# Gate, up and conv projections of a split-float32 decoder kernel: two activation parts in one 512-column matmul

## The chip, the cores and the metric

One core of a Trainium2 chip. The metric is device microseconds of one execution. The kernel is compared with itself after one change.

## The reference, cut to what matters

The model is two layers of [half SwiGLU FFN, parallel token mixing, half SwiGLU FFN] over 256 tokens of width 1024, all in float32, with one RMSNorm at the end.

```
def swiglu(h, wg, wu, wd):
    return (jax.nn.silu(h @ wg) * (h @ wu)) @ wd
...
for l in range(2):
    x = x + 0.5 * swiglu(rms_norm(x, ffn1_norm[l]), ffn1_wg[l], ffn1_wu[l], ffn1_wd[l])
    z = rms_norm(x, mix_norm[l]) @ w_in[l]     # retention, block attention, conv: a, gate
    ...                                        # u = a * sigmoid(gate), then the depthwise conv
    x = x + mix @ w_out[l]
    x = x + 0.5 * swiglu(rms_norm(x, ffn2_norm[l]), ffn2_wg[l], ffn2_wu[l], ffn2_wd[l])
return rms_norm(x, final_norm)
```

The FFN is 2816 wide, that is 22 tiles of 128; the conv branch has 256 channels and a gate of 256.

## The kernel before, in words

**Products.** Each float32 operand is split into a float32r high part and a float32r remainder ("hi" and "lo"), and a product is the sum of three passes: hi times hi, hi times lo, lo times hi. All three accumulate in PSUM.

**Weights.** They arrive as one stream of units of up to 1 MB, in the order of use, through three "raw" buffers filled from SyncE's queue (L125). `pump` splits the next half unit: ScalarE copies it to a "whi" piece (L145) and VectorE subtracts to get "wlo" (L146). Ten pieces of each exist (`WBUFS`). `take` hands pieces to the products and `free` returns them.

**Order.** TensorE runs in the order in which the code emits its work. `tick` follows each group of products; it pumps one half unit and advances side chains, which are generators that wait for some number of ticks before their next TensorE work. In the stretches where the order is not written out by hand (`ordered(False)`: most of an FFN, and the mixing from the conv projections on) a planner places the work of ScalarE and VectorE; in the others they too run as emitted.

**An FFN** (`ffn`, four times). `first_pair` (L407) makes the first two tiles with the activations as the stationary operand and 512 columns of weights streaming (L201 to L203). Its result is transposed (L401) into a bank of the tag "tr" called `pt` and split from there (L404). Then ten pairs of `single` (L416): 20 tiles, each with a gate half and an up half of 8 steps over the inner dimension. A step is `mm3w` (L205 to L209): three matmuls of 256 columns, with the weights (whi, whi, wlo) as the stationary operand and the activations (hThi, hTlo, hThi) streaming. Gate and up are written to the two column halves of one bank of the tag "mm", which has two banks, as has "tr"; "acc" has four. Behind the up half ScalarE takes the Silu of the gate from PSUM (L428), VectorE multiplies by the up half from PSUM (L429), and the product is split (L430, in L196 and L197). From the third tile pair on, each pair of `single` is followed by two `down` blocks for tiles of the pair before the last (L433 to L445): 512 columns of weights streaming past the split product. The last four tiles go through `down` in a tail (L469 to L473), and the residual is added (L475).

**The mixing** (`mix`, twice). It starts with two attention projections (`chunk`, L488, 384 columns each), then `glu` (L658) makes the conv branch's gate and value with `mm3w`, into "acc" banks: two rounds of 8 steps for each of two channel tiles. Gate: Sigmoid on ScalarE (L674); value: a product on VectorE into `u` (L676). Then 31 taps of depthwise convolution run on VectorE (L686, L688) under the other projections, and TensorE transposes the result (L694). The output projection is `outp` (L768 to L781), 512 columns of weights streaming.

**Activations.** `new_hT` (L361) makes two tiles, "hThi" and "hTlo", each 128 x 8 x 256; `norm_T` (L345) fills them from transposes. The last norm (`Final`, L899) uses one buffer of each tag for its two row tiles (L905, L906).

Of the kernel before, what the change touches and what calls it, by code (L numbers as in the profile page):

```python
# [11 lines left out]
F32 = mybir.dt.float32  # L12
F32R = mybir.dt.float32r
BF16 = mybir.dt.bfloat16
I32 = mybir.dt.int32
AF = mybir.ActivationFunctionType
OP = mybir.AluOpType
AX = mybir.AxisListType
PSUM = bass.MemoryType.PSUM

D = 1024
S = 256
P = 128
L = 2
KT = D // P
NT = S // P
# [4 lines left out]
HW = H * HD  # L31
# [12 lines left out]
NVEC = OFF_BT + 2 * L  # L44


# Float32 products run as three float32r passes: every operand is split exactly into a
# float32r high part and a float32r remainder, and hi*hi + hi*lo + lo*hi accumulate in PSUM.
#
# Weights arrive as one stream of units in the order of use. `pump` splits the next half unit  # L50
# into a rotating set of hi/lo pieces, `take` hands pieces to the products, `free` gives them
# back. TensorE runs in emission order; `tick` follows every group of products and advances
# the side chains (generators that yield the number of ticks, or the condition, to wait for
# before their next TensorE work), so that their latency hides behind the products.
class Kernel:
    def __init__(self, ctx, tc, a, out):
        self.tc, self.nc, self.a, self.out = tc, tc.nc, a, out
# [24 lines left out]
    def bank(self, tag, bufs):  # L82
        return self.ps.tile([P, 512], F32, tag=tag, bufs=bufs, name=self.name(tag))
# [118 lines left out]
        mm(out, ah, wl, start=False, stop=False)  # L202
        mm(out, al, wh, start=False, stop=stop)  # L203

    def mm3w(self, out, wh, wl, xh, xl, start, stop):  # L205
        mm = self.nc.tensor.matmul
        mm(out, wh, xh, start=start, stop=False)  # L207
        mm(out, wh, xl, start=False, stop=False)  # L208
        mm(out, wl, xh, start=False, stop=stop)  # L209

    def load(self, name, shape, dt=F32, eng=None):
        t = self.const.tile(list(shape), dt, tag=name, name=name)
# [146 lines left out]
        return g  # L359

    def new_hT(self):  # L361
        hi = self.act.tile([P, KT, S], F32R, tag="hThi", bufs=2, name=self.name("hThi"))
        lo = self.act.tile([P, KT, S], F32R, tag="hTlo", bufs=2, name=self.name("hTlo"))
        return hi, lo

    def projA(self, ps, t, hT, pieces, n, free):
        kk = KT // len(pieces)
# [11 lines left out]
    def ffn(self, f, cur, nxt):  # L379
        nc = self.nc  # L380
        hT = cur.hT
        ys = [[self.acc() for _ in range(2)] for _ in range(NT)]
        with self.tc.tile_pool(name=f"ffn{f}", bufs=1) as fp:
            hf = {}

            def new_hf(j):
                hi = fp.tile([P, S], F32R, tag="hfh", bufs=TAIL + 4, name=self.name("hfh"))
                lo = fp.tile([P, S], F32R, tag="hfl", bufs=TAIL + 4, name=self.name("hfl"))
                hf[j] = (hi, lo)
                return hf[j]  # L390

            def new_sh():
                return [fp.tile([P, 256], F32, tag=x, bufs=2, name=self.name(x)) for x in "sh"]
# [20 lines left out]
                    self.spawn(gated(t, ps, pt))  # L414

            def single(j):  # L416
                ps = self.mmb()
                s, h = new_sh()
                for gu in range(2):
                    (w,) = self.take(1)  # L420
                    wh, wl = [x.rearrange("p (k n) -> p k n", k=KT) for x in w]
                    for k in range(KT):
                        self.mm3w(ps[:, gu * S:(gu + 1) * S], wh[:, k], wl[:, k], hT[0][:, k], hT[1][:, k], k == 0, k == KT - 1)
                        if k == 3:
                            self.tick()
                    self.free()
                    if gu == 1:
                        nc.scalar.activation(s, ps[:, 0:S], AF.Silu)  # L428
                        nc.vector.tensor_tensor(h, s, ps[:, S:2 * S], op=OP.mult)  # L429
                        self.split(*new_hf(j), h)  # L430
                    self.tick()

# [17 lines left out]
            for p in range(1, FT // 2):  # L450
                single(2 * p)
                single(2 * p + 1)
                if p == 1:
                    self.need(f"pair{f}")
                if p > 1:
                    for j in (2 * p - 4, 2 * p - 3):
                        (w,) = self.take(1)
                        for t in range(NT):
                            down(j, t, w)
                            if t == 1:  # L460
                                self.free()
                            self.tick()
                if f == 0 and p == 2:
                    self.setup_late()
                if f == 0 and p == 4:
                    self.spawn(self.tables())
# [12 lines left out]
    def mix(self, l, cur, nxt):  # L479
        nc, a = self.nc, self.a  # L480
        hT = cur.hT
        mT = self.new_hT()
        with self.tc.tile_pool(name=f"mix{l}", bufs=1) as mp:

            def tl(tag, shape, bufs=1):
                return mp.tile(shape, F32, tag=tag, bufs=bufs, name=self.name(tag))

            def chunk(w, t, free):  # L488
                ps = self.mmb()
                self.projA(ps, t, hT, w, HW, free)  # L490
                return ps[:, :HW]
# [166 lines left out]
            def glu():  # L658
                for i in range(2):
                    w = [[x.rearrange("p (k n) -> p k n", k=4) for x in hl] for hl in self.take(2)]  # L660
                    ps = [self.acc()[:, :S] for _ in range(2)]
                    for k in range(KT):
                        wh, wl = w[k // 4]
                        for ct in range(2):
                            cs = slice(ct * P, (ct + 1) * P)
                            self.mm3w(ps[ct], wh[:, k % 4, cs], wl[:, k % 4, cs], hT[0][:, k], hT[1][:, k], k == 0, k == KT - 1)
                        if k % 4 == 3:
                            self.free()
                        if k % 2:
                            self.tick()  # L670
                    for ct in range(2):
                        g = sg[:, ct * S:(ct + 1) * S]
                        if i == 0:
                            nc.scalar.activation(g, ps[ct], AF.Sigmoid)  # L674
                        else:
                            nc.vector.tensor_tensor(u[:, ct, pad:], g, ps[ct], op=OP.mult)  # L676

            def conv():
                for j in range(TAPS):
# [43 lines left out]
            pad = TAPS - 1  # L723
            sg = tl("sg", [P, 512])
            u = tl("u", [P, 2, pad + S])
# [15 lines left out]
            w = self.take(4)  # L741
# [4 lines left out]
            w = self.take(4)  # L746
            for t in range(NT):
                self.spawn(rot(chunk(w, t, t == 1), t, rqT, "rq"))
            w = self.take(4)
            for t in range(NT):  # L750
                self.spawn(rot(chunk(w, t, t == 1), t, rkT, "rk"))
            w = self.take(4)
            rv = [values("rv", chunk(w, t, t == 1)) for t in range(NT)]
            w = self.take(4)
# [3 lines left out]
            for t in range(NT):  # L758
                ps = chunk(w, t, t == 1)
                v = tl("rg", [P, HW], 2)  # L760
# [4 lines left out]
            mm = nc.tensor.matmul  # L765
# [88 lines left out]
class Into:  # L854
# [9 lines left out]
    def state(self, t):  # L864
        k = self.k
        if t == 0:
            self.hT = k.new_hT()
        return {"tile": lambda: k.act.tile([P, D], F32, tag="xr", bufs=1, name=k.name("xr"))}
# [30 lines left out]
class Final(Into):  # L899
# [2 lines left out]

    def state(self, t):
        k = self.k
        tag = "hThi" if t == 0 else "hTlo"  # L905
        return {"tile": lambda: k.act.tile([P, KT * S], F32, tag=tag, bufs=2, name=k.name("y"))[:, :D]}  # L906

    def finish(self, t, n):
        k = self.k
# [67 lines left out]
```

## Time and profile before

| | |
|---|---|
| median of 3 runs | 1013.67 us (1013.66 to 1014.0) |
| span of the profiled execution | 1013.2 us |
| its own time | not recorded beside the span; the median lies 0.5 us above the span |
| matmuls, and weight loads | 6656 each |
| read from memory | 178.74 MB, 177 GB/s over the span |

The profile is one execution. PE is TensorE's matmuls, PEld its weight loads, DVE VectorE, ACT ScalarE, POOL GpSimd, SP SyncE. A row "L207 PE MATMUL mm<-hThi,whi" is an instruction of line 207 that writes a tile of tag mm from hThi and whi. Matmuls are pipelined, so the duration of one row is longer than the distance to the next one's start; the distance between starts is what a matmul costs in a stream. Times on the timeline are microseconds from the span's start.

### The profile page before, as it was taken

How to read it: one execution, taken by the hardware profiler on the slowest of the kernel's cores; microseconds unless marked ns; L12 is line 12 of the kernel's file. 1: busy time of each engine (PE TensorE's matmuls, PEld its weight loads, DVE VectorE, ACT ScalarE, POOL GpSimd, SP SyncE). 2: the span in 40 equal slices, each digit the busy share in tenths (PEclk: the TensorE clock that was granted, in tenths of full speed). 3: DMA queues.
4: the chain of work that ended last, by engine and by line, in shares of the span. 5: the costliest groups of instructions: out<-in, count | busy, mean ns of one | idle time of the engine just before them, and what ended most of it. 6: DMA issues, size and time to landing. Idle time of an engine off the chain costs nothing.

```text
span 1013.2 us, 16088 instructions
## 1 busy us (share of the span) xinstructions
PE 993.9 (98%) x6656; PEld 920.0 (91%) x6656; DVE 625.2 (62%) x864; ACT 483.2 (48%) x736; POOL 66.0 (7%) x109
## 2 busy tenths in 40 slices
PE   5999999999999999999999999999999999999997
PEld 4999999898998999999889999998989889999995
DVE  6875555469976755555575555546699676555542
ACT  5644444356554644444364444444565455444432
POOL 1010000021140000000000000002101400000000
PEclk9999999999999999999999999999999999999999
DMA  9955554436541755545446455543535346555511
GB/s 304 340 191 202 169 202 150 146 118 201 180 167 66 299 196 173 202 169 197 175 172 219 171 194 181 185 148 136 186 136 195 139 155 240 187 188 177 199 42 42
DMA packets 28729, 180.83 MB, mean 178 GB/s; under 512 B 3440, under 2 KB 3824, under 8 KB 10480
## 3 DMA queue, kind: packets, MB, share of 16 engines
q1 hardware_dynamic: 27360, 176.07, 48.9%
q10 hardware_dynamic: 1296, 3.74, 1.0%
q8 instruction: 52, 0.85, 0.3%
q14 instruction: 21, 0.17, 0.0%
HBM read 178.74 MB, written 1.05 MB: 177 GB/s over the span
## 4 chain that ended last, share of the span: by engine, by line
PE 94%; DMA 2%; DVE 2%; ACT 1%; issue 1%; POOL 0%; SPq 0%; POOLq 0%; ACTq 0%; DVEq 0%
PE mm L207 15%; PE mm L209 15%; PE mm L208 15%; PE acc L445 8%; PE acc L441 8%; PE acc L442 8%; PE mm L201 5%; PE mm L203 4%; PE mm L202 4%; PE tr L349 1%; DMA raw<-in_win 1%; PE acc L582 1%; PE acc L632 1%; PE acc L209 1%; PE acc L207 1%; PE acc L208 1%
## 5 line engine op out<-in xcount | busy, mean ns | idle before, releaser
L146 DVE TENSOR_TENSOR wlo<-raw,whi 128x1024 fp32r<-128x1024 f32 (+2 forms) x348 | 403.7, 1172 | 271.6 <-ACT whi L145 271.3
L145 ACT ACTIVATE whi<-raw 128x1024 fp32r<-128x1024 f32 (+2 forms) x348 | 347.7, 1011 | 294.9 <-PE mm L208 179.8
L207 PE MATMUL mm<-hThi,whi 128*128 128x256 f32 x1280 | 362.5, 283 | 0.0
L209 PE MATMUL mm<-hThi,wlo 128*128 128x256 f32 x1280 | 362.0, 283 | 0.0
L208 PE MATMUL mm<-hTlo,whi 128*128 128x256 f32 x1280 | 362.0, 283 | 0.0
L208 PEld LDWEIGHTS mm<-hTlo,whi 128*128 128x128 f32 x1280 | 245.3, 192 | 1.7
L207 PEld LDWEIGHTS mm<-hThi,whi 128*128 128x128 f32 x1280 | 245.2, 192 | 1.6
L209 PEld LDWEIGHTS mm<-hThi,wlo 128*128 128x128 f32 x1280 | 245.3, 192 | 0.0
L441 PE MATMUL acc<-whi,hfh 128*128 128x512 f32 x352 | 139.4, 396 | 0.0
L442 PE MATMUL acc<-wlo,hfh 128*128 128x512 f32 x352 | 138.6, 394 | 0.0
L445 PE MATMUL acc<-whi,hfl 128*128 128x512 f32 x352 | 115.7, 395 | 0.0
L201 PE MATMUL mm<-whi,hThi 128*128 128x384 f32 (+1 forms) x288 | 106.1, 368 | 0.5 <-ACT whi L145 0.5
L202 PE MATMUL mm<-wlo,hThi 128*128 128x384 f32 (+1 forms) x288 | 100.5, 349 | 0.5 <-DVE wlo L146 0.5
L203 PE MATMUL mm<-whi,hTlo 128*128 128x384 f32 (+1 forms) x288 | 100.6, 349 | 0.0
L196 ACT ACTIVATE hfh<-h 128x256 fp32r<-128x256 f32 x80 | 33.4, 418 | 100.1 <-DVE h L429 100.0
L445 PEld LDWEIGHTS acc<-whi,hfl 128*128 128x128 f32 x352 | 66.1, 188 | 15.1
L442 PEld LDWEIGHTS acc<-wlo,hfh 128*128 128x128 f32 x352 | 66.3, 188 | 14.0
L441 PEld LDWEIGHTS acc<-whi,hfh 128*128 128x128 f32 x352 | 66.6, 189 | 13.6
L201 PEld LDWEIGHTS mm<-whi,hThi 128*128 128x128 f32 x288 | 54.4, 189 | 5.3 <-issue 1.3
L202 PEld LDWEIGHTS mm<-wlo,hThi 128*128 128x128 f32 x288 | 54.4, 189 | 3.5 <-DVE wlo L146 1.3
L688 DVE SCALAR_TENSOR_TENSOR ac<-u,vec,ac 128x256 f32<-128x256 f32 x120 | 57.1, 529 | 0.0
L203 PEld LDWEIGHTS mm<-whi,hTlo 128*128 128x128 f32 x288 | 54.1, 188 | 2.7 <-DVE hTlo L197 0.2
(145 smaller groups left out, 712.8 us busy)
## 6 DMA issues: line engine op xcount, KB each, us to landing
raw<-in_wgb SPq DMA_DIRECT2D x80, 1024.0 KB, 4.8
raw<-in_wd SPq DMA_DIRECT2D x44, 1024.0 KB, 4.8
raw<-in_win SPq DMA_DIRECT2D x28, 768.0 KB, 4.4
raw<-in_wout SPq DMA_DIRECT2D x8, 1024.0 KB, 4.7
raw<-in_wga SPq DMA_DIRECT2D x6, 1024.0 KB, 4.8
raw<-in_wcv SPq DMA_DIRECT2D x4, 1024.0 KB, 4.7
raw<-in_wga SPq DMA_DIRECT2D x8, 256.0 KB, 7.1
g<-in_fgain ACTq DMA_DIRECT2D x3, 512.0 KB, 3.4
```

The lines of the kernel that those rows point to most:

```text
L145: nc.scalar.activation(hi[:, c], src, AF.Copy)
L146: nc.vector.tensor_tensor(lo[:, c], src, hi[:, c].bitcast(F32), op=OP.subtract)
L201: mm(out, ah, wh, start=start, stop=False)
L202: mm(out, ah, wl, start=False, stop=False)
L203: mm(out, al, wh, start=False, stop=stop)
L207: mm(out, wh, xh, start=start, stop=False)
L208: mm(out, wh, xl, start=False, stop=False)
L209: mm(out, wl, xh, start=False, stop=stop)
L441: mm(ys[t][h], hi[:, ts], wh[:, n], start=first, stop=False)
L442: mm(ys[t][h], hi[:, ts], wl[:, n], start=False, stop=False)
L445: mm(ys[t][h], lo[:, ts], wh[:, n], start=False, stop=last)
L688: nc.vector.scalar_tensor_tensor(ac[ct], us, wj, ac[ct], op0=OP.mult, op1=OP.add)
```

## The change

A step over the inner dimension is now `mm2w`: one matmul of 512 columns that streams both activation parts past whi, into both column halves of a bank, and one of 256 columns that streams the high part past wlo, into the first half. The low half of the bank is added to the first half outside TensorE: `joined` copies it to SBUF on ScalarE and adds on VectorE. Gate and up take a bank each, gate of tag "mm" and up of tag "tr"; `glu` uses whole "acc" banks. High and low parts of the activations become one tile, and the last norm's two row tiles one tile of the same tag.

```diff
-    def mm3w(self, out, wh, wl, xh, xl, start, stop):
+    def mm2w(self, out, wh, wl, x, start, stop):
         mm = self.nc.tensor.matmul
-        mm(out, wh, xh, start=start, stop=False)
-        mm(out, wh, xl, start=False, stop=False)
-        mm(out, wl, xh, start=False, stop=stop)
+        mm(out, wh, x, start=start, stop=False)
+        mm(out[:, :S], wl, x[:, 0], start=False, stop=stop)
+
+    def joined(self, new, ps):
+        lo, v = new(), new()
+        self.nc.scalar.activation(lo, ps[:, S:], AF.Copy)
+        self.nc.vector.tensor_tensor(v, lo, ps[:, :S], op=OP.add)
+        return v
...
     def new_hT(self):
-        hi = self.act.tile([P, KT, S], F32R, tag="hThi", bufs=2, name=self.name("hThi"))
-        lo = self.act.tile([P, KT, S], F32R, tag="hTlo", bufs=2, name=self.name("hTlo"))
-        return hi, lo
+        both = self.act.tile([P, KT, 2, S], F32R, tag="hT", bufs=2, name=self.name("hT"))
+        return both[:, :, 0], both[:, :, 1], both
...
             def single(j):
-                ps = self.mmb()
                 s, h = new_sh()
-                for gu in range(2):
+                for gu, bank in enumerate((self.mmb, self.trb)):
+                    ps = bank()
                     (w,) = self.take(1)
                     wh, wl = [x.rearrange("p (k n) -> p k n", k=KT) for x in w]
                     for k in range(KT):
-                        self.mm3w(ps[:, gu * S:(gu + 1) * S], wh[:, k], wl[:, k], hT[0][:, k], hT[1][:, k], k == 0, k == KT - 1)
+                        self.mm2w(ps, wh[:, k], wl[:, k], hT[2][:, k], k == 0, k == KT - 1)
                         if k == 3:
                             self.tick()
                     self.free()
-                    if gu == 1:
-                        nc.scalar.activation(s, ps[:, 0:S], AF.Silu)
-                        nc.vector.tensor_tensor(h, s, ps[:, S:2 * S], op=OP.mult)
+                    v = self.joined(lambda: fp.tile([P, S], F32, tag="part", bufs=4, name=self.name("part")), ps)
+                    if gu == 0:
+                        nc.scalar.activation(s, v, AF.Silu)
+                    else:
+                        nc.vector.tensor_tensor(h, s, v, op=OP.mult)
                         self.split(*new_hf(j), h)
                     self.tick()
...
             def glu():
...
-                    ps = [self.acc()[:, :S] for _ in range(2)]
+                    ps = [self.acc() for _ in range(2)]
...
-                            self.mm3w(ps[ct], wh[:, k % 4, cs], wl[:, k % 4, cs], hT[0][:, k], hT[1][:, k], k == 0, k == KT - 1)
+                            self.mm2w(ps[ct], wh[:, k % 4, cs], wl[:, k % 4, cs], hT[2][:, k], k == 0, k == KT - 1)
...
                         g = sg[:, ct * S:(ct + 1) * S]
+                        v = self.joined(lambda: tl("w", [P, HW], 5)[:, :S], ps[ct])
                         if i == 0:
-                            nc.scalar.activation(g, ps[ct], AF.Sigmoid)
+                            nc.scalar.activation(g, v, AF.Sigmoid)
                         else:
-                            nc.vector.tensor_tensor(u[:, ct, pad:], g, ps[ct], op=OP.mult)
+                            nc.vector.tensor_tensor(u[:, ct, pad:], g, v, op=OP.mult)
...
     def state(self, t):
         k = self.k
-        tag = "hThi" if t == 0 else "hTlo"
-        return {"tile": lambda: k.act.tile([P, KT * S], F32, tag=tag, bufs=2, name=k.name("y"))[:, :D]}
+        if t == 0:
+            self.y = k.act.tile([P, NT, D], F32, tag="hT", bufs=2, name=k.name("y"))
+        return {"tile": lambda: self.y[:, t]}
```

## Rows read from the trace of the kernel before

**Rows 1.** The page's head: span, then busy us, share and instructions.

```profile
span 1013.2 us, 16088 instructions
...
PE 993.9 (98%) x6656; PEld 920.0 (91%) x6656; DVE 625.2 (62%) x864; ACT 483.2 (48%) x736; POOL 66.0 (7%) x109
```

**Rows 2.** The chain that ended last, by engine.

```profile
PE 94%; DMA 2%; DVE 2%; ACT 1%; issue 1%; POOL 0%; SPq 0%; POOLq 0%; ACTq 0%; DVEq 0%
```

**Rows 3.** TensorE's waits: waiter, releaser, us in total, times, longest.

```profile
PE tr L349 <- DVE xr L343: 9.6, 3, 9.1
PE tr L499 <- POOL w L512: 2.1, 2, 1.4
```

**Rows 4.** Groups by line and shape, TensorE: count, busy us, mean ns, idle.

```profile
L207 PE MATMUL mm<-hThi,whi 128*128 128x256 f32 x1280 | 362.5, 283 | 0.0
...
L207 PE MATMUL acc<-hThi,whi 128*128 128x256 f32 x64 | 18.4, 288 | 0.0
```

**Rows 5.** Timeline of a single, TensorE: start, us; 27 matmuls of 256 columns.

```profile
79.83 0.28 PE L207 MATMUL mm<-hThi,whi 128*128 128x256 f32 x1
79.95 0.28 PE L208 MATMUL mm<-hTlo,whi 128*128 128x256 f32 x1
...
82.95 0.28 PE L209 MATMUL mm<-hThi,wlo 128*128 128x256 f32 x1
```

**Rows 6.** Table by stretch: PE, PEld, DVE, ACT, POOL busy; clock, DMA share, GB/s.

```profile
77.20:94.20 17.00, 17.00 (x122) 15.95 (x121) 8.86 (x10) 7.51 (x10) 0.00 (x0) 1.00 0.51 179
...
20.00:40.00 20.00, 20.00 (x147) 18.96 (x147) 17.98 (x21) 15.47 (x22) 0.00 (x0) 1.00 0.92 332
```

**Rows 7.** Timeline of a 384-column projection; the second starts nine matmuls later.

```profile
230.32 0.33 PE L201 MATMUL mm<-whi,hThi 128*128 128x384 f32 x1
...
231.88 0.33 PE L201 MATMUL mm<-whi,hThi 128*128 128x384 f32 x1
```

**Rows 8.** Timeline of the output projection, 512 columns; six matmuls apart.

```profile
308.13 0.39 PE L777 MATMUL acc<-whi,hThi 128*128 128x512 f32 x1
...
309.49 0.39 PE L777 MATMUL acc<-whi,hThi 128*128 128x512 f32 x1
```

**Rows 9.** Timeline of a first pair, 512 columns; ten matmuls apart.

```profile
516.60 0.39 PE L202 MATMUL mm<-wlo,hThi 128*128 128x512 f32 x1
...
518.90 0.39 PE L203 MATMUL mm<-whi,hTlo 128*128 128x512 f32 x1
```

**Rows 10.** Timeline of a down block, 512 columns; six matmuls between the first two.

```profile
84.46 0.40 PE L441 MATMUL acc<-whi,hfh 128*128 128x512 f32 x1
...
85.85 0.40 PE L441 MATMUL acc<-whi,hfh 128*128 128x512 f32 x1
86.09 0.40 PE L442 MATMUL acc<-wlo,hfh 128*128 128x512 f32 x1
```

**Rows 11.** Lines 428 and 429: ns min/median/max, first and last start us.

```profile
L428 ACT ACTIVATE s<-mm x80: 363/366/386, 33.2 to 989.9; 128x256 f32<-128x256 f32 x80
...
L429 DVE TENSOR_TENSOR h<-s,mm x80: 410/415/422, 34.5 to 990.3; 128x256 f32<-128x256 f32 x80
```

**Rows 12.** Line 145: what ScalarE's idle time before a split ended on.

```profile
  PE mm L208: 179.8, 106
```

**Rows 13.** Timeline, TensorE: three single starts.

```profile
289.89 0.60 PE L694 MATMUL tr<-ident,ac 128*128 128x128 f32 x4
...
332.46 0.28 PE L207 MATMUL mm<-hThi,whi 128*128 128x256 f32 x1
...
997.32 0.40 PE L441 MATMUL acc<-whi,hfh 128*128 128x512 f32 x1
```

**Rows 14.** Timeline, VectorE: the work that those starts stand behind.

```profile
287.20 0.47 DVE L688 SCALAR_TENSOR_TENSOR ac<-u,vec,ac 128x256 f32<-128x256 f32 x1
...
341.99 0.42 DVE L197 TENSOR_TENSOR hfl<-tr,hfh 128x256 fp32r<-128x256 f32 x1
...
991.24 0.43 DVE L197 TENSOR_TENSOR hfl<-h,hfh 128x256 fp32r<-128x256 f32 x1 [0.48 <-ACT hfh L196]
```

## The prediction

> **What bounds the kernel now.** I read the head of the page first: TensorE's matmuls are busy for 98% of a span of 1013.2 us, VectorE for 62%, ScalarE for 48% [rows 1]. A busy TensorE could still be one that others hold up, so the chain of waits comes next: 94% of it is TensorE's own work [rows 2]. Then TensorE's waits: 9.6 us in the start-up and 2.1 us behind a rotation on GpSimd, and almost nothing else [rows 3]. So TensorE's stream of matmuls sets the time, and what counts is the distance between two starts, not the duration in a row.
>
> The change touches the three-matmul steps: 1280 in the FFNs and 64 in the conv projections, one matmul of each step per row [rows 4]. That makes 1344 steps. In a single, 26 distances between starts take 82.95 − 79.83 = 3.12 us: 120.0 ns for each 256-column matmul, 360 ns for a step [rows 5]. This is 1344 x 360 = 484 us, nearly half of the span. The granted clock is 1.00 there, the level of 2.4 GHz [rows 6].
>
> **Does a wide matmul cost as much as two narrow ones?** The columns that stream don't change: 3 x 256 before, 512 + 256 after. Only a part of the cost that comes once per instruction can be saved, so I look for it in the distances at other widths. Nine matmuls of 384 columns take 231.88 − 230.32 = 1.56 us, 173.3 ns each [rows 7]. Six of 512 in the output projection take 1.36 us, 226.7 ns each [rows 8]. So 256, 384 and 512 columns cost 120.0, 173.3 and 226.7: each 128 columns add 53.3 ns, and 13.3 ns are left over per instruction, each of which here has its own weight load. The change takes one matmul and one weight load out of each step.
>
> Two rows speak for a smaller gain. In a first pair ten matmuls of 512 columns take 2.30 us, 230 ns each [rows 9], and in a down block six take 85.85 − 84.46 = 1.39 us, 232 ns each [rows 10]. Which is nearest to the new instruction? It pairs an activation tile hT with a weight piece; so do the output projection (mT, from the same function) and the first pair, while the down block pairs weights with the split products. I take the middle of the first two, 228.5 ns, and keep 226.7 and 232 as ends. A step then costs 228.5 + 120.0 = 348.5 ns, 11.5 less than before. **Saved on TensorE: 1344 x 11.5 = 15.5 us** (17.9 at one end, 10.7 at the other).
>
> By the Trainium skill, "TensorE: Matmul & The Clock Gate", section "Back-to-back issue gap", a warm stream costs N/2.4 + 2.5 ns, which would put the fixed part at 2.5 ns and the saving, an estimate, at 1344 x 2.5 = 3.4 us. The rows of this case have 13.3 ns over the same per-column cost, and the sum goes by them.
>
> **What is added.** Each gate and up half gets a ScalarE copy out of PSUM and a VectorE addition that reads PSUM: 160 of each in the FFNs and 8 in the conv projections, 168. The kernel has no such copy; nearest is the Silu of a 256-column half from PSUM, 0.366 us, and for the addition the product with a PSUM half, 0.415 us [rows 11]. That is 61 us on ScalarE and 70 us on VectorE over the whole kernel, on no path by itself. In a steady stretch of two singles and their down blocks, 17.0 us, VectorE is busy for 8.86 us and ScalarE for 7.51 [rows 6]. Four sums bring these to 10.5 and 9.0 of some 16.6 us: the cover is there. The other cover is the lead of the weight splits: ScalarE's waits before a split end mostly on TensorE giving a piece back, 179.8 us in 106 waits on line 208 alone [rows 12], so ten pieces stand ready. A copy that waits for the end of a half holds up the splits placed behind it on ScalarE, and VectorE's part of them in turn, by up to the 2.8 us of a half, while each piece in the lead lasts as long or longer. If that lead were gone, TensorE would wait for both.
>
> **Where the sums could be late.** Three places.
> (a) *Products for the tail.* The last single's split ends at 991.24 + 0.43 = 991.67, and the tail first needs it at 997.32 [rows 13, 14]: 5.6 us, against 0.8 us more work. Nothing.
> (b) *Conv.* The last tap ends at 287.67, its transposes start at 289.89 [rows 13, 14]: 2.2 us. The input `u` comes later by a copy and an addition for each channel tile, up to 1.6 us. Nothing, bound 1 us in each layer.
> (c) *The first two singles of an FFN.* The up half now takes a "tr" bank. Of the two, one still holds `pt` until its second split is read. In the second FFN the singles start at 332.46 and the second single's up half would start three halves of 2.79 us later, at 340.8; that split ends at 341.99 + 0.42 = 342.41 [rows 13, 14]. If TensorE must have that bank it waits 1.6 us; I let it stand for all four, so 6.4 us is a bound. The other bank is the first single's up half, free after its copy and addition. I take 0.4 us for each FFN, since each of the two sums can stand behind a weight split on its engine: **1.5 us in all**, between 0 and 6.4.
>
> The start of the first FFN is the fullest stretch: VectorE 17.98 and ScalarE 15.47 us of 20 [rows 6]. Two singles' sums there add 1.7 and 1.5 us. VectorE would just fit; TensorE has pieces in hand by then. I cost it inside (c).
>
> DMA: no transfer is added or moved, SyncE's queue keeps its order, and raw buffers come free with the splits. The steady stretch moves 179 GB/s where the start-up moved 332 [rows 6], so the 1.5% higher rate is hidden. One tile for hi and lo makes the first wide matmul wait for both parts, which the old second matmul of the step, 0.12 us later, did anyhow. The final norm's common tile is costed at nothing: the two halves are different columns; if the second had to wait for the first's transfer, some 1 us.
>
> **Sum.** The span 1013.2 and the 0.5 us between it and the median make 1013.7. 1013.7 − 15.5 + 1.5 = **999.7 us**. Low end: 1013.7 − 17.9 = 995.8. High end: 1013.7 − 10.7 + 3 = 1006.
>
> **Rivals.**
> 1. *Fast matmuls, but the banks hold TensorE.* The low saving together with (c) and (b) in full: 1013.7 − 10.7 + 6.4 = 1009.4. For it: `pt` is read late in the trace. Against: another bank of the tag is free sooner. Chance 0.05 for 1006 to 1011.
> 2. *The wide instruction costs as much as two narrow ones*, because it streams two halves, or is issued as two. A distance of 240 ns, twice 120, stands in a down block: 86.09 − 85.85 [rows 10]. Then nothing is saved: 1013.7. Against: such a distance is rare, and the output projection's 226.7 is steady; rows of 512 columns are single instructions. Chance 0.03. The skill's rule named above lies near this, at 1010.3 by its estimate; the trace's 13.3 ns disagree with it. Chance 0.03.
> 3. *Slower: the sums stand on TensorE's path.* A copy waiting for its half delays the splits placed behind it, and if the lead of ten pieces drains in the singles, every sum costs TensorE 0.366 + 0.415 = 0.78 us: 168 x 0.78 = 131 us, so 1013.7 − 15.5 + 131 = 1129. It decides from 15.5/168 = 0.09 us of exposed time per sum. For it: VectorE's and ScalarE's load at an FFN's start. Against: half of their steady time is idle [rows 6], and the waits of rows 12. Chance 0.05.
>
> **How the numbers follow.** My case has 0.84 and lies between 995.5 and 1006, which is also the range; rival 1 and the skill's rule lie above it, rival 2 and 3 further out. A measurement of this kernel can tell about 0.2%, 2 us, from no change: faster 0.84 + 0.05 + 0.03 = 0.92, the same 0.03, slower 0.05.
>
> **What the profile after would show.** 5312 matmuls and weight loads instead of 6656. In a single, a wide start followed 0.227 to 0.232 us later by a narrow one, and 0.12 us later by the next wide one. Pairs of singles shorter by 32 x 11.5 ns = 0.37 us. ScalarE up by about 61 us and VectorE by 70. TensorE's waits unchanged but for a few of a microsecond or less in the first two singles of an FFN. Wrong would be: a wide step of 0.24, waits of matmuls for weight splits or for the new copies in every pair, or VectorE near its whole time in the steady stretch.

## The result, and the profile after

The changed kernel takes 1000.46 us (median of four runs, 1000.15 to 1000.97) against 1013.71 (1013.66 to 1014.00) for the kernel before: a ratio of 0.9866, 95% interval 0.9854 to 0.9878. That is 1.3% less; the prediction took 0.2% for what can be told from no change. The forecast was 999.7 in 995.5 to 1006.

The head of the page after answers to [rows 1], and the next line, the chain by engine, to [rows 2]:

```profile
span 998.4 us, 13763 instructions
...
PE 981.6 (98%) x5312; PEld 847.6 (85%) x5312; DVE 685.5 (69%) x1032; ACT 537.9 (54%) x904; POOL 64.1 (6%) x109
...
PE 90%; DVE 6%; DMA 1%; ACT 1%; issue 1%; SPq 0%; POOL 0%; POOLq 0%; ACTq 0%; DVEq 0%
```

TensorE is busy for the same 98%, with 1344 matmuls and 1344 weight loads fewer. VectorE has 60 us more and ScalarE 55, and the span is 15 us shorter all the same (13.5 against a second trace of before, experiment 5): they had the room. The chain is still TensorE's. VectorE's share of it rises from 2 to 6%: in both mixes it goes back from a late `q` through VectorE's taps and weight splits (223 to 246 us in the first).

TensorE's waits after (waiter, releaser, us in total, times, longest) answer to [rows 3]:

```profile
PE tr L354 <- DVE xr L348: 8.5, 3, 8.1
PE acc L588 <- ACT q L578: 0.8, 2, 0.4
PE mm L201 <- ACT hT L196: 0.7, 1, 0.7
PE tr L207 <- DVE hfl L197: 0.2, 1, 0.2
```

The first wait is the start-up's, as before. The one behind GpSimd's rotation is gone; 0.8 us in the attention, where a transposed `q` is late, has come instead. The last row is the wait that the prediction priced at 1.5 us: it is 0.2 in this execution, at one instruction.

The groups of TensorE and of the two new operations (count, busy us, mean ns, idle before) answer to [rows 4, 11]:

```profile
L207 PE MATMUL mm<-hT,whi 128*128 128x512 f32 x640 | 227.3, 396 | 0.0
...
L208 PE MATMUL mm<-hT,wlo 128*128 128x256 f32 x640 | 178.7, 279 | 0.0
...
L212 ACT ACTIVATE part<-mm 128x256 f32<-128x256 f32 x80 | 29.3, 366 | 6.8 <-PE mm L208 6.8
...
L213 DVE TENSOR_TENSOR part<-part,mm 128x256 f32<-128x256 f32 x80 | 33.1, 414 | 2.9 <-ACT part L212 2.9
```

The copy and the addition take 366 and 414 ns, what the prediction took for them from their neighbours. The durations of all rows add up to 67 us more on ScalarE (62 of them for the copies, 4 for a longer Silu) and 70 on VectorE. Busy time rises by less, 54.7 and 60.3, since rows overlap and overlapping time counts once: on ScalarE one copy starts at 57.25 behind a split that runs from 56.28 to 57.34.

Where did TensorE's time go? The timeline of TensorE's starts (start, duration in us) through one pair of singles, from its first wide matmul to the first of its down block, in the middle of the FFN:

```profile
53.42 0.40 PE L207 MATMUL mm<-hT,whi 128*128 128x512 f32 x1
...
61.74 0.39 PE L207 MATMUL tr<-hT,whi 128*128 128x512 f32 x1
61.98 0.27 PE L208 MATMUL tr<-hT,wlo 128*128 128x256 f32 x1
62.09 0.40 PE L207 MATMUL tr<-hT,whi 128*128 128x512 f32 x1
...
64.52 0.39 PE L447 MATMUL acc<-whi,hfh 128*128 128x512 f32 x1
```

That is 32 steps in 64.52 − 53.42 = 11.10 us, 346.9 ns a step: better than the 348.5 forecast. The next pair in the same view is not as short:

```profile
70.08 0.39 PE L207 MATMUL mm<-hT,whi 128*128 128x512 f32 x1
...
76.67 0.28 PE L208 MATMUL mm<-hT,wlo 128*128 128x256 f32 x1
76.78 0.40 PE L207 MATMUL mm<-hT,whi 128*128 128x512 f32 x1
77.02 0.28 PE L208 MATMUL mm<-hT,wlo 128*128 128x256 f32 x1
77.13 0.40 PE L207 MATMUL mm<-hT,whi 128*128 128x512 f32 x1
...
81.38 0.39 PE L447 MATMUL acc<-whi,hfh 128*128 128x512 f32 x1
```

81.38 − 70.08 = 11.30 us, 353.1 ns a step. Of the 32 pairs of singles that stand between two down blocks, eight in each FFN, 16 are short and 16 long, taking turns within an FFN. The mean is 350, so a step saves 360 − 350 = 10 ns: in a step of 350 the narrow matmul follows after some 234 ns and the next wide one after some 116 (on the mean 231.9 and 114.8 in the short pairs, 236.1 and 116.7 in the long).

The table by stretch (busy us of PE, PEld, DVE, ACT, POOL with counts; clock, DMA share, GB/s) for these two stretches and for the start of the first FFN answers to [rows 6]:

```profile
53.42:70.08 16.66, 16.66 (x89) 14.23 (x88) 14.10 (x38) 8.66 (x14) 0.00 (x0) 1.00 0.56 190
70.08:86.95 16.87, 16.87 (x89) 14.34 (x88) 13.24 (x28) 9.24 (x16) 2.26 (x8) 1.00 0.51 178
20.00:40.00 20.00, 20.00 (x111) 17.24 (x110) 18.42 (x24) 16.71 (x26) 0.00 (x0) 1.00 0.90 324
```

TensorE's column equals the length in all three, at a granted clock of 1.00, so neither waits nor the clock make the two kinds. In the first two stretches VectorE also has the work of the rotary tables; even so it leaves 2.5 us free. In the third it is busy for 18.42 of 20 us, and TensorE still does not wait.

### The profile page after: what moved, and what is told of

The parts are those of the page before. It is cut to its first block, busy times and chain, and to the rows that moved or that the text cites. A ratio compares the mean times of both kernels' runs of the same rounds, so it can differ in the third digit from the quotient of the medians.

```text
span 998.4 us, 13763 instructions
## 1 busy us (share of the span) xinstructions
PE 981.6 (98%) x5312; PEld 847.6 (85%) x5312; DVE 685.5 (69%) x1032; ACT 537.9 (54%) x904; POOL 64.1 (6%) x109
## 4 chain that ended last, share of the span: by engine, by line
PE 90%; DVE 6%; DMA 1%; ACT 1%; issue 1%; SPq 0%; POOL 0%; POOLq 0%; ACTq 0%; DVEq 0%
PE tr L207 15%; PE mm L207 15%; PE acc L451 8%; PE acc L448 8%; PE acc L447 8%; PE tr L208 7%; PE mm L208 7%; PE mm L201 4%; PE mm L202 4%; PE mm L203 4%; DVE wlo L146 3%; DVE ac L695 2%; PE acc L207 1%; PE tr L354 1%; PE acc L638 1%
## 5 line engine op out<-in xcount | busy, mean ns | idle before, releaser
L207 PE MATMUL tr<-hT,whi 128*128 128x512 f32 x640 | 228.0, 397 | 0.2 <-DVE hfl L197 0.2
L207 PE MATMUL mm<-hT,whi 128*128 128x512 f32 x640 | 227.3, 396 | 0.0
L208 PE MATMUL mm<-hT,wlo 128*128 128x256 f32 x640 | 178.7, 279 | 0.0
L208 PE MATMUL tr<-hT,wlo 128*128 128x256 f32 x640 | 178.7, 279 | 0.0
L207 PEld LDWEIGHTS tr<-hT,whi 128*128 128x128 f32 x640 | 120.2, 188 | 29.2 <-PE mm L208 0.4
L207 PEld LDWEIGHTS mm<-hT,whi 128*128 128x128 f32 x640 | 120.2, 188 | 28.5
L208 PEld LDWEIGHTS mm<-hT,wlo 128*128 128x128 f32 x640 | 120.6, 189 | 1.5
L208 PEld LDWEIGHTS tr<-hT,wlo 128*128 128x128 f32 x640 | 120.7, 189 | 0.0
L201 PE MATMUL mm<-whi,hT 128*128 128x384 f32 (+1 forms) x288 | 106.7, 371 | 0.7 <-ACT hT L196 0.7
L203 PE MATMUL mm<-whi,hT 128*128 128x384 f32 (+1 forms) x288 | 101.2, 351 | 0.0
L202 PE MATMUL mm<-wlo,hT 128*128 128x384 f32 (+1 forms) x288 | 101.1, 351 | 0.0
L201 PEld LDWEIGHTS mm<-whi,hT 128*128 128x128 f32 x288 | 54.7, 190 | 5.5 <-issue 1.3
```

The source lines that it names most:

```text
L201: mm(out, ah, wh, start=start, stop=False)
L207: mm(out, wh, x, start=start, stop=False)
L208: mm(out[:, :S], wl, x[:, 0], start=False, stop=stop)
```

## The experiments

The theory: the time comes from the width alone, and the sums lie beside it. The rivals: the other banks or the order bring it; or the sums take part of it back. Ratios are to the kernel before on the same chip.

**1. The change without its width.** The high and low parts go as two matmuls again, but into the two column halves, with the banks, the common tile and the sums of the change. The first step of each half, which starts the accumulation of both column halves, stays wide: 168 of the 1344 steps.

```diff
     def mm2w(self, out, wh, wl, x, start, stop):
-        mm(out, wh, x, start=start, stop=False)
+        if start:
+            mm(out, wh, x, start=True, stop=False)
+        else:
+            mm(out[:, :S], wh, x[:, 0], start=False, stop=False)
+            mm(out[:, S:], wh, x[:, 1], start=False, stop=False)
```

> The changed kernel, but in 1176 of the 1344 steps (all except the first of each half) the 512-column matmul is two of 256 columns into the two halves of the same bank; banks, sums and activation tile stay as in the change. Theory (a matmul and its weight load have a fixed cost, and the change saves one of each per step): a step costs 360 ns again instead of the 350.6 read in the changed kernel's trace, so 1000.5 + 1176 x 0.0094 = 1011.5 us, give or take 1. Rival (the gain comes from giving gate and up a bank each and from the new order of the other engines' work, not from the width): stays within 1 us of 1000.5.

Measured: 1012.81 us (1012.61 to 1013.68), before 1013.85, ratio 0.999 (0.9981 to 0.9999). Nine starts of its timeline:

```profile
55.74 0.28 PE L210 MATMUL mm<-hT,whi 128*128 128x256 f32 x1
55.86 0.28 PE L211 MATMUL mm<-hT,whi 128*128 128x256 f32 x1
55.98 0.28 PE L212 MATMUL mm<-hT,wlo 128*128 128x256 f32 x1
...
56.82 0.28 PE L210 MATMUL mm<-hT,whi 128*128 128x256 f32 x1
```

(56.82 − 55.74) / 9 = 120.0 ns, the distance of [rows 5] again. The time is 1.3 us above the theory's 1011.5: 12.35/1176 is 10.5 ns for each step made narrow, where 9.4 were taken. The 1.0 us that is left of the saving is about what its 168 wide steps save at 10 ns, 1.7 us. So the banks, the tile and the order are worth nothing that can be seen, and some 12 of the 13 us hang on the width.

**2. The change without the sums.** What follows reads the high-part columns alone, so the low part of the activations drops out of the result.

```diff
-                    v = self.joined(lambda: fp.tile(...), ps)
+                    v = ps[:, :S]
...
-                        v = self.joined(lambda: tl("w", [P, HW], 5)[:, :S], ps[ct])
+                        v = ps[ct][:, :S]
```

> The changed kernel without the 168 copies and additions: Silu, Sigmoid and products read the first half of the bank, and the product of high weights and low activations is left out of the result. Theory (the sums lie beside TensorE's work): 1000.5 us, give or take 1. Rival (part of each sum stands on TensorE's path, which is why the gain is 13.2 us and not the 17.9 of the narrowest fixed cost): faster by what the sums cost, 996 to 998 us.

Measured: 1001.03 us (1000.66 to 1002.3), ratio 0.9876 (0.9859 to 0.9892). Its head of the page:

```profile
PE 981.9 (98%) x5312; PEld 847.0 (85%) x5312; DVE 623.3 (62%) x864; ACT 483.3 (48%) x736; POOL 69.3 (7%) x109
```

ScalarE and VectorE are back at the busy times of [rows 1], and the time does not fall. The sums cost nothing that can be seen. 20 of the 32 pairs are short here against 16, which alone is worth 0.8 us, so less than about a microsecond can't be told.

**3. The sums twice.** After each sum a second copy and a second VectorE operation (a maximum of two equal values) stand in the path of the result. The tag "part" gets eight buffers in place of four.

```diff
         self.nc.vector.tensor_tensor(v, lo, ps[:, :S], op=OP.add)
-        return v
+        lo2, v2 = new(), new()
+        self.nc.scalar.activation(lo2, v, AF.Copy)
+        self.nc.vector.tensor_tensor(v2, lo2, v, op=OP.max)
+        return v2
```

> The changed kernel with each sum followed by a second copy on ScalarE and a second two-input operation on VectorE in series (a maximum of the sum and its copy, which leaves the value as it is). It adds another 61 us of ScalarE, 70 us of VectorE, and over 0.8 us of delay to each sum. Theory (covered by idle time and by the lead of the weight splits): 1000.5 us, at most 1.5 more, and that in the first singles of the FFNs. Rival (the cover is thin, so that sums come onto TensorE's path): 10 us more or worse.

Measured: 1002.74 us (1001.75 to 1003.86), ratio 0.9889 (0.9874 to 0.9903): 2.3 us above the change for 51 us more on VectorE (736.1 us busy) and 47 more on ScalarE (584.6). TensorE's waits other than the start-up's:

```profile
PE tr L508 <- POOL w L521: 2.2, 2, 1.1
...
PE acc L454 <- DVE hfl L197: 0.2, 1, 0.2
```

The forecast of at most 1.5 us, in the first singles of the FFNs, was too low and named the wrong place. From the conv projection to the next FFN the two mixes take 119.9 and 119.8 us, against 119.2 each in the change and 119.4 without sums. The wait at the rotation on GpSimd stands there, but it was 2.1 and 1.3 us in two traces of before too, so that the sums bring it is not shown. In the FFNs, where 160 of the 168 sums are, one matmul waits 0.2 us. The cover of the FFNs holds twice the work.

**4. A step's worth, reversed once in each pair.** The second step of each pair as three narrow matmuls, to price what one step gives.

```diff
                     for k in range(KT):
-                        self.mm2w(ps, wh[:, k], wl[:, k], hT[2][:, k], k == 0, k == KT - 1)
+                        if (j % 2, gu, k) == (0, 0, 1):
+                            mm, x = nc.tensor.matmul, hT[2][:, k]
+                            mm(ps[:, :S], wh[:, k], x[:, 0], start=False, stop=False)
+                            mm(ps[:, S:], wh[:, k], x[:, 1], start=False, stop=False)
+                            mm(ps[:, :S], wl[:, k], x[:, 0], start=False, stop=False)
+                        else:
+                            self.mm2w(ps, wh[:, k], wl[:, k], hT[2][:, k], k == 0, k == KT - 1)
```

> The changed kernel with the second step of every pair of singles made with three 256-column matmuls, which is 40 more matmuls of about 10 ns each, 0.4 us in all. In the changed kernel's trace pairs alternate between two kinds, 347 ns and 353 to 354 ns for a step. Theory (the kind is set by the point in time at which a pair's stream begins, and one more matmul shifts it): the order of the kinds changes, and the time goes to somewhere between 997.5 (all pairs of the short kind) and 1004 us (all long). Rival (it is set by something else that alternates from pair to pair, such as buffers or the other engines' work): pairs alternate as before, and 1000.9 us.

Measured: 1004.61 us (1003.74 to 1004.96), ratio 0.9905 (0.9891 to 0.992). Forty matmuls more cost 4.15 us, 104 ns for each, not ten. The timeline shows why: pair, down block, next pair:

```profile
87.79 0.39 PE L207 MATMUL mm<-hT,whi 128*128 128x512 f32 x1
...
99.09 0.39 PE L453 MATMUL acc<-whi,hfh 128*128 128x512 f32 x1
...
104.65 0.39 PE L207 MATMUL mm<-hT,whi 128*128 128x512 f32 x1
```

99.09 − 87.79 = 11.30, and so are all 32 pairs. With one step at 360, the other 31 take 353: the edit has turned the 16 short pairs long, 16 x 0.20 = 3.2 us, and its own ten nanoseconds are the small part.

**5. The kernel before, once more,** for a second profiled execution, since the first one's own time was not recorded.

> The kernel before, unchanged, to have its profiled execution's own time beside its span. In the first trace of it the span (1013.2 us) lay 0.5 us under the median of the runs; in the changed kernel and in the four kernels made from it the span lies 1.8 us under the same execution's time. Theory (1.8 us lie around the span in every execution, and the traced execution of before was one of the longer ones): time minus span is 1.8 us, span about 1012. Rival (the change lengthened what lies around the span): 0.5 us, span about 1013.2.

Measured: 1014.09 us, beside 1013.76 for the same kernel's other runs (ratio 1.0003, 0.9994 to 1.0012); its profiled execution took 1013.72 with a span of 1011.9. Time and span lie 1.8 us apart, as in the change (1000.19 and 998.4); in experiment 2 it is 2.1. The first trace of before, with 1013.2, was thus probably of an execution longer than the ones timed beside it, by about a microsecond. Its head and its waits, beside [rows 1, 3]:

```profile
span 1011.9 us, 16088 instructions
...
PE tr L349 <- DVE xr L343: 9.0, 3, 8.6
PE tr L499 <- POOL w L512: 1.3, 2, 0.9
```

The wait at the rotation is 1.3 here against 2.1: it differs by 0.8 between executions of one kernel. The stages from this trace, by the starts of the first matmul of each:

| stretch | before, us | after, us | saved |
|---|---|---|---|
| start to the first FFN's singles | 25.1 | 25.4 | −0.2 |
| first FFN, to the conv projection | 187.0 | 183.7 | 3.3 |
| to the next FFN | 120.0 | 119.2 | 0.8 |
| second FFN, to the third | 189.7 | 186.3 | 3.4 |
| third FFN, to the conv projection | 187.0 | 184.2 | 2.9 |
| to the next FFN | 119.6 | 119.2 | 0.4 |
| fourth FFN, to the end | 183.5 | 180.5 | 3.0 |

The last column is taken before rounding. Each FFN has 320 steps: 2.9 to 3.4 us are 9 to 11 ns a step. The saving is where the steps are.

**6. The wide matmul alone.** The product with the weights' low part is left out, so nothing stands between two wide matmuls.

```diff
     def mm2w(self, out, wh, wl, x, start, stop):
-        mm(out, wh, x, start=start, stop=False)
-        mm(out[:, :S], wl, x[:, 0], start=False, stop=stop)
+        mm(out, wh, x, start=start, stop=stop)
```

> The changed kernel without the 256-column matmul of each step, so the product of low weights and high activations is left out of the result: only 512-column matmuls with one weight load each. The gain of the change depends on what a 512-column matmul costs in a row of such; the trace of before had 226.7 ns in the output projection and 232 in the down blocks. Theory A (operands decide: an activation tile against weight pieces gives 226.7): 1344 x (350.6 - 226.7) less, 834 us. Theory B (any long row of 512-column matmuls in these FFNs slips as the down blocks do): 232 ns, 841 us. Under both the whole is nearer to the bound of the other engines' work, so waits on weight splits may hide the difference in the time; it is read from the distances between starts.

Measured: 845.22 us (843.61 to 846.04), ratio 0.8338 (0.8324 to 0.8352). Halves of eight matmuls on its timeline, after two starts of the down block ahead of them, six matmuls apart:

```profile
58.25 0.40 PE L446 MATMUL acc<-whi,hfh 128*128 128x512 f32 x1
...
59.64 0.39 PE L446 MATMUL acc<-whi,hfh 128*128 128x512 f32 x1
...
62.44 1.99 PE L207 MATMUL mm<-hT,whi 128*128 128x512 f32 x8
64.27 1.98 PE L207 MATMUL tr<-hT,whi 128*128 128x512 f32 x8
66.08 1.98 PE L207 MATMUL mm<-hT,whi 128*128 128x512 f32 x8
67.89 1.98 PE L207 MATMUL tr<-hT,whi 128*128 128x512 f32 x8
69.71 0.40 PE L446 MATMUL acc<-whi,hfh 128*128 128x512 f32 x1
```

(69.71 − 62.44) / 32 = 227 ns for a wide matmul of the singles; (59.64 − 58.25) / 6 = 232 for one of the down block, a few microseconds earlier in the same kernel. So the instruction itself is as cheap as the low end of the forecast, [rows 8]; it is the turn of wide and narrow that makes 234 and 116 of it. Without the narrow half, the singles are short enough for the banks to come late:

```profile
PE tr L207 <- DVE part L212: 3.4, 2, 2.5
PE tr L207 <- DVE hfl L197: 1.6, 2, 1.0
```

These are the waits of the prediction's place (c): for the addition (L212 in this kernel) and for the second split of `pt`. They stand one step beyond the change: with 1344 matmuls of some 115 ns fewer, 5.0 us; with them, 0.2. They are also about half of the 11 us by which the time lies above theory A's 834; for the rest no row is named here.

**7. Three narrow matmuls at the head of the pairs that were short, or at the end.** Two theories for the kinds: any odd step makes a pair long; or what a pair's end leaves behind decides the next one. The edit is experiment 4's, with another condition, in the steady pairs (from the third or the fourth on):

```diff
-                        if (j % 2, gu, k) == (0, 0, 1):
+                        if (j % 2, gu, k) == (0, 0, 1) and j >= (4 if f < 2 else 6):
```

> The changed kernel with the second step of a pair of singles made with three 256-column matmuls in the pairs from the third tile pair on (first two FFNs) or from the fourth (last two), which are the first places where the changed kernel's own pairs are of the short kind or would become so. Without the additional matmul a short pair was followed by a long one and a long by a short; with it (the kernel with one more in every pair) a long one was followed by a long one. Theory (the point in time at which a pair's stream begins decides, and one more matmul undoes the turn): a short pair is followed by a short one, nearly all pairs short, about 1000.5 - 14 x 0.19 + 0.4 = 998.2 us. Rival (three narrow matmuls at the head always lead to the long kind): 1004 us.

Measured: 1004.19 us (1003.14 to 1005.97), ratio 0.9905 (0.989 to 0.992); 3 pairs short, 29 long, so the rival held, but for the first of the eight pairs in three FFNs. At the end instead:

```diff
+                        if (j % 2, gu, k) == (1, 1, 6) and j >= (4 if f < 2 else 6):
```

> As the run before, but the step made with three matmuls is the last but one of the pair, so that it cannot touch the kind of the pair that it stands in, only what follows. Theory: nearly all pairs short, about 998.2 us. Rival (the head of the pair decides): alternation as in the changed kernel, 1000.9 us.

Measured: 998.99 us (998.18 to 1000.6), ratio 0.9854 (0.9839 to 0.9869); 29 pairs short, 3 long; the three are again first pairs, and the 28 others are all short. The same extra matmul, put at the pair's end and not at its head, gives 5.2 us between two kernels of equal work on the same chip; there are 26 more short pairs, 26 x 0.20 = 5.2 us.

**8. The change again, and the extra matmul at the end of all pairs,** on one chip:

> The changed kernel once more, unchanged, so that the kernel with one more matmul at each pair's end is compared with it on the same chip. Theory (the kind of a pair is set by the order of the matmuls before it and is the same in every execution): half of the 32 pairs from the third tile pair on short, half long, in turn, 1000.5 us. Rival (it falls out anew in each execution): another count of short pairs, and a time that goes with it, 997.5 to 1004.

> The changed kernel with the last but one step of every pair of singles, the first ones of an FFN too, made with three 256-column matmuls: 40 more matmuls. In the run with this from the third or fourth tile pair on, every pair behind such an end was short. Theory (the end of a pair decides on the next): all 32 pairs from the third tile pair on short, 1.5 to 2.5 us faster than the changed kernel on the same chip, about 998.5 us. Rival (those 29 of 32 were chance, the difference of 1.5 us noise): the same as the changed kernel, 1000.5 us.

The condition of the second is `(j % 2, gu, k) == (1, 1, 6)` alone. Measured: 1000.91 us (1000.39 to 1001.57) for the change, ratio 0.9869 (0.9853 to 0.9886), with 18 pairs short and 14 long; 999.81 (999.15 to 1000.95), ratio 0.9861 (0.9847 to 0.9876), with 29 short and 3 long. Pairs of the latter:

```profile
87.80 0.40 PE L207 MATMUL mm<-hT,whi 128*128 128x512 f32 x1
...
98.91 0.39 PE L453 MATMUL acc<-whi,hfh 128*128 128x512 f32 x1
...
104.48 0.40 PE L207 MATMUL mm<-hT,whi 128*128 128x512 f32 x1
...
121.17 0.40 PE L207 MATMUL mm<-hT,whi 128*128 128x512 f32 x1
```

98.91 − 87.80 = 11.11 us with a step of 360 in it, and 16.69 us from pair to pair. In the change's second trace the rival held: two FFNs begin with two short pairs, where the first trace has none that do. From the second pair of an FFN on the kinds take turns in both. So the order of the matmuls alone does not set the kind.

With the edit at the end the forecast of 32 short pairs was missed by three, all first pairs of an FFN behind such an end; in experiment 7 one such pair, in the first FFN, was long too, which the expectation overlooked. For the 28 pairs that are not first, the durations settle that the edit at the end keeps them short. Its 1.1 us against the change do not settle that it is a faster kernel: the intervals overlap. The 11 pairs that are short in addition save 11 x 0.20 = 2.2 us, and the forty narrow steps take back some 0.4 at 10 ns each, so 1.8 would be expected, and a change of 0.2% is about what can be told from none.

A clean steady pair of the change's second profile, with no table work on VectorE (columns as in the table by stretch above):

```profile
357.90:374.60 16.70, 16.70 (x89) 14.31 (x88) 10.47 (x15) 8.89 (x14) 0.00 (x0) 1.00 0.52 179
```

**9. Is it the place of the tiles, or what the down block reads?** One kernel pads the FFN pool with a tile of 16 KB in each partition, to shift the tiles:

```diff
+            pad = fp.tile([P, 4096], F32, tag="pad", bufs=1, name=self.name("pad"))
+            nc.gpsimd.memset(pad[:, 0:8], 0.0)
```

> The changed kernel with 16 KB per partition of unused memory in the pool of the FFN, so that the split products (and the other tiles of that pool) lie elsewhere. The down blocks take 232 ns for a 512-column matmul where the output projection, with the same order and activations of the tag hT, takes 227. Theory (where the stationary operand lies in memory decides): the down blocks' distance changes, at best to 227, and the time to 994.5 us. Rival (the place doesn't matter): 232 ns and 1000.5 us.

Measured: 1001.41 us (1001.04 to 1002.18), ratio 0.9877 (0.9862 to 0.9892). Its down block, 24 matmuls:

```profile
82.88 0.39 PE L449 MATMUL acc<-whi,hfh 128*128 128x512 f32 x1
...
88.44 0.39 PE L207 MATMUL mm<-hT,whi 128*128 128x512 f32 x1
```

5.56 / 24 = 232 ns, as ever, with 19 pairs short and 13 long. With the pad nothing changes; that it moved the tiles is taken from the code, and no trace shows it. The other kernel lets the down block multiply by columns of the activation tile, in place of the split products:

```diff
-                    mm(ys[t][h], hi[:, ts], wh[:, n], start=first, stop=False)
+                    mm(ys[t][h], hT[0][:, j % KT, ts], wh[:, n], start=first, stop=False)
...
-                    mm(ys[t][h], lo[:, ts], wh[:, n], start=False, stop=last)
+                    mm(ys[t][h], hT[1][:, j % KT, ts], wh[:, n], start=False, stop=last)
```

> The changed kernel with the down blocks' stationary operand taken from the FFN's input activations hT instead of the split products, in the same order and number; the result is then another product, and the split products are made but not used. Theory (the operands decide what a 512-column matmul costs): 227 ns as in the output projection, 1056 x 5.5 ns = 5.8 us less, 994.7 us. Rival (the row of 24 matmuls slips whatever it reads): 232 ns, 1000.5 us.

Measured: 1000.54 us (999.11 to 1001.1), ratio 0.9865 (0.9851 to 0.988). The same view:

```profile
82.83 0.40 PE L447 MATMUL acc<-whi,hT 128*128 128x512 f32 x1
...
88.33 0.39 PE L207 MATMUL mm<-hT,whi 128*128 128x512 f32 x1
```

5.50 / 24 = 229 ns, between theory and rival: the operand of the down block is part of why its matmuls stand wider apart. But all 32 pairs are long here: 16 more than in the change cost 16 x 0.20 = 3.2 us, about what 1056 matmuls save at 3 ns, and the time is the change's. An edit of the down block alone thus changes the kind of the singles around it; by what means, no run here shows.

## Why the prediction was right, point by point

**What bounds the kernel** was right: the saving appears FFN by FFN in proportion to the steps (table in experiment 5), and without the width it is gone (experiment 1).

**The saving on TensorE** was forecast at 1344 x 11.5 = 15.5 us and measures 1344 x 10 = 13.4. The term that was mis-sized is the step of 348.5 ns: the mean is 350. The reading was that each matmul of the new stream keeps the distance that its width has elsewhere, 228.5 and 120. Neither does. Alone the wide one has 227 (experiment 6), in turn with narrow ones some 234; the narrow one has 116. The two errors, 5.5 ns too low and 4 too high, leave 1.5 by luck, so the forecast of the step was better than its parts. The two rows behind 228.5 stream weights past activations, and the new matmul does the reverse; no row of before had that at 512 columns. And the step is not one number: 346.9 or 353.1, by the pair, so that a pair became shorter by 0.41 or 0.22 us where 0.37 was forecast.

**The fixed part per matmul** (13.3 ns over the 53.3 per 128 columns) gave the 17.9 us at the far end of the forecast, a third more than the 13.4 measured; 10 ns per matmul removed is what is left of it. By the Trainium skill, "TensorE: Matmul & The Clock Gate", section "Back-to-back issue gap", 2.5 ns over N/2.4 is the fixed part of an isolated warm gap; the prediction took it for that of a stream. For this stream the runs disagree with it, since 1344 times 2.5 ns is 3.4 us and 13.25 were measured. The same section says that in a stream of weight loads and matmuls both set the spacing; that fits a stream in which the removed matmul took a weight load with it, but no run here parts the two.

**The sums on ScalarE and VectorE** at nothing: right to within about a microsecond (experiment 2), and with room to spare in the FFNs (experiment 3). Their durations were right to a nanosecond or two, and the forecast of a steady stretch, 10.5 us on VectorE and 9.0 on ScalarE, came out at 10.47 and 8.89 (experiment 8).

**The waits** of place (c) were put at 1.5 us in all and are 0.2. The step that failed is the guess of 0.4 us for every FFN: in this execution the banks come in time in three of four. In the traces of experiments 4 and 7 to 9 the waits on line 207 add up to between 0 and 0.8 us. That the mechanism exists, and how near it was, experiment 6 shows. It went the other way from the error in the step, and so by luck the total, −14.0 forecast and −13.25 measured, is closer than either part.

**Places (a) and (b) and the last norm's common tile** were put at nothing: no wait of TensorE stands at the tail or at the conv's transposes, and the last stretch of the table, with the norm in it, saves 3.0 us as the other FFNs do. What the forecast of the profile did not have is the 0.8 us for `q` in place of the 2.1 at the rotation.

**The sum's starting point.** The median lay 0.5 us above the traced span of before, and the prediction took that as the time around the span. It is 1.8 (experiment 5); the trace was probably of a longer execution. As the sum ended at the median all the same, nothing followed from it but that terms read from that trace may be about a microsecond large.

**The rivals.** A wide matmul that costs two narrow ones is excluded by 227 ns in experiment 6. The banks hold TensorE for 0.2 us. Sums on TensorE's path are excluded by experiment 2.

## What to carry to other kernels

Where TensorE is the bound and two products share a stationary operand, stream both in one matmul and add the halves elsewhere: each matmul removed here gave 10 ns, and engines with idle time took 168 sums at no cost that can be seen. Price it from the distance between starts at several widths in the same trace, and leave room for a mixed stream: here the distances of 512 and 256 columns alone, 227 and 120 ns, add up to 347, and a step of both takes 350. Before testing one step's worth by adding an instruction, look at the distances around it: here one more instruction in a pair changed the distances in all of it.

## What the runs showed of the hardware beyond that

- A stream that alternates 512 and 256 columns runs at one of two steady rates, 346.9 or 353.1 ns a step, for a whole pair of 32 steps, at a granted clock of 1.00 and without waits. With a step of three narrow matmuls at the end of the pairs 29 of 32 are short, with it at their head 29 or 32 of 32 are long (experiments 4, 7 and 8). Why there are two rates stays open.
- The distance of 512-column matmuls depends on their operands and on what runs around them: 227 alone in the singles, 232 in the down block between them, 229 in that block with another operand (experiments 6 and 9).
- The Silu of a 256-column half reads the sum from SBUF now and takes longer than it did from PSUM, 414 ns against 366 [rows 11]:

```profile
L433 ACT ACTIVATE s<-part 128x256 f32<-128x256 f32 x80 | 33.2, 414 | 79.2 <-DVE part L213 79.1
```
